# A 64-byte wider constant tile, a token scaling on VectorE and a later place for the gate projections, in a one-core hybrid encoder layer

## The chip, the cores and the metric

The kernel runs on 1 core of one Trainium2 chip. The metric is the device time of one execution in microseconds (us); 0.2% of it is about what a measurement of this kernel can tell from no change. Engines are named as in the profile: PE is TensorE (PEld its loads of the resident operand), DVE is VectorE, ACT is ScalarE, POOL is GpSimd, SP is the engine that issues the transfers (DMA).

## The reference

One layer over 1024 tokens of width 1024, in float32: a mixer of window attention and a gated delta rule (DeltaNet) on one input projection, a cross attention into 256 memory tokens, and a SwiGLU network of width 2816. Each has an RMS norm before and after it.

```python
h = _rms_norm(x, g_mix_pre[l])
proj = h @ w_in[l]
aq, ak, av, dqkv, dgate, dalpha, dbeta = jnp.split(proj, IN_SPLITS, axis=-1)
...
mix = jnp.concatenate([attn_o, dn_o], axis=-1) @ w_out[l]
x = x + _rms_norm(mix, g_mix_post[l])
c = _memory_cross_attention(_rms_norm(x, g_cross_pre[l]), _rms_norm(mem, g_mem[l]),
                            w_cq[l], w_ckv[l], w_co[l])
x = x + _rms_norm(c, g_cross_post[l])
f = _swiglu(_rms_norm(x, g_ffn_pre[l]), w_gate_up[l], w_down[l])
x = x + _rms_norm(f, g_ffn_post[l])
```

`dgate` is the gate of the DeltaNet output: `o * silu(gate)`, needed only when the delta rule has run over a token.

## The kernel before

**Number format.** Every float32 operand of a large product is split in a high and a low part (`split`: ScalarE casts the high part at L102, VectorE or GpSimd subtracts it for the low part at L103), and a product is three matmuls: high by high, high by low, low by high. Nearly all of them stream an operand of 128x512 past a resident one of 128x128. In the profile `pg<-hhi,whi` means: into the PSUM tile pg, streamed hhi, resident whi.

**Memory.** Tiles are allocated in pools, on the left side of the on-chip memory, upwards from address 0, or on the right side, downwards from the end. The pool `cst` holds constants and is the first on the left; behind it come `wp`, with the raw weights `wraw` and their parts `whi` and `wlo`, and everything that is opened later: `b0` to `b3` (tokens of the later stages and the cross attention's queries), `cph` (its probabilities), `x22` and `bhi` (the SwiGLU product), `dhl` and `t4h` (the down product). On the right lie `hhi`, `hlo` (the transposed input), `s0` (again transposed tokens) and `s0h` to `s3l` (sums of weights). `phalf` is a constant that the kernel fills and does not read.

**Stages.** (1) Norm and transposition of x. (2) Input projection (`pg`, L261), tile by tile of 128 output columns; beside it the DeltaNet preparation: `base_inverse` inverts 32x32 triangles in a chain of short VectorE operations (L534, L536, ending at L538 and L539), `levels` builds larger inverses out of them with small matmuls (L576 to L591); `attn_proj` multiplies queries and keys by cosine and sine (L729, L730, L735) and stores them; `value_proj` and `gate_proj` do the value and the gates; `window` computes window attention (`psw`, L633). (3) `scan` steps the delta rule over chunks of 128 tokens, with memory keys and values and further windows as filler. (4) `mid_gemm` (`pmg`, L1016) multiplies by `w_out`, twice for 512 tokens each, then the mid norm: residual added (L1030), sum of squares (L1033), the root on GpSimd (L162), and the token tile scaled by it (L1036). (5) Cross attention: queries `pcq` (L261), scores `pcs` (L1097), output `pco` (L1123), and `mid_gemm` by `w_co`, again twice. (6) SwiGLU: gate and up product (L1191) by a scheme with seven block products, and the down product (`block_product`, L1381, and L1474).

**What sets the order.** The work of stage (2) is issued by strings: `ORDER_1` for DeltaNet, `ORDER_2` for what follows. In them `D` is a DeltaNet projection, `P` its preparation, `B` a `base_inverse`, `L` a `levels`, `A` an `attn_proj` (A4 is the keys), `V` the `value_proj`, `G` a `gate_proj`, `W` a group of windows. The order of issue is a priority: a scheduler places each instruction on its engine's queue as early as its inputs, its tiles and the engine allow by a model of durations, so work from several stages is interleaved. The place in the queue is fixed when the program is built. All transfers are issued by the SP queue. `load_w` raises the priority of loading and splitting weights. The window pool `tw` and the levels' pool reuse memory that the second `base_inverse` holds until it ends.

The token tile is scaled before the change by

```python
nc.scalar.activation(xr, z, AF.Identity, scale=r2)
```

and the tile xr is then transposed by TensorE for the next product.

Of the kernel before, what the change touches and what calls it, by code (L numbers as in the profile page):

```python
# [10 lines left out]
F32 = mybir.dt.float32  # L11
F32R = mybir.dt.float32r
I32 = mybir.dt.int32
AF = mybir.ActivationFunctionType
ALU = mybir.AluOpType
# [4 lines left out]
P = 128  # L20
# [13 lines left out]


ORDER_1 = "D0 P0 D1 P1 D2 B0 P2 D3 P3 B1".split()
ORDER_2 = "L0 L1 G0 G1 A4 V A0 A1 L2 L3 W W W A2 A3 G2 G3 W".split()
ORDER_3 = ("M " + "s01 W K " * 5 + "s01 K " * 3 + "s01 V V").split()


# [35 lines left out]
def tile_hybrid_block(  # L76
# [6 lines left out]
    nc = tc.nc  # L83
# [4 lines left out]
    if dump is None:  # L88
        def dump(name, ap):
            pass  # L90
# [17 lines left out]
    def pool(name, bufs, **kw):  # L108
        return tc.tile_pool(name=name, bufs=bufs, reuse_waits="tile", **kw)

    cst = ctx.enter_context(pool("cst", 1))
# [6 lines left out]
    def load_w(src, k, n, eng=None, after=None):  # L118

        with tc.high_priority(AHEAD):  # L120
            raw = wp.tile([P, k, n], F32, tag="wraw", name="wraw")
            with ExitStack() as order_:
                if after:
                    order_.enter_context(tc.issue_after(after.ins))
                nc.sync.dma_start(raw, src.rearrange("(k p) n -> p k n", p=P))
            hi = wp.tile([P, k, n], F32R, tag="whi", name="whi")
            lo = wp.tile([P, k, n], F32R, tag="wlo", name="wlo")
            split(hi, lo, raw, eng=eng)
        return hi, lo
# [2 lines left out]
    ident = cst.tile([P, P], F32, name="ident")  # L132
    mhalf = cst.tile([P, 16], F32, name="mhalf")
    nc.gpsimd.memset(mhalf, -0.5)
    phalf = cst.tile([P, 16], F32, name="phalf")
    nc.gpsimd.memset(phalf, 0.5)
    cols = cst.tile([P, P], F32, name="cols")
    p12 = ExitStack()
# [19 lines left out]
    def rstd_of(rs, ss, n, eps):  # L158

        w = ss.shape[-1]  # L160
        nc.gpsimd.tensor_scalar(rs, ss, n, eps, ALU.mult, ALU.add)
        nc.gpsimd.tensor_tensor(rs, rs, mhalf[:, :w], ALU.pow)  # L162
# [540 lines left out]
    def issue(order, table):  # L703
        for o in order:
            table[o[0]](*(int(c) for c in o[1:]))
# [54 lines left out]

    issue(ORDER_2, {"A": attn_proj, "V": value_proj, "G": gate_proj, "L": levels, "W": next_windows})
    dump("d_q", d_q); dump("d_k", d_k); dump("d_gate", d_gate)
# [202 lines left out]
    L0 = ExitStack()  # L965
# [33 lines left out]
    def mid_gemm(tz, act, w, gp, res, dst, hf, between=None):  # L999


        zs = [tz.tile([P, D], F32, tag="z", name="z", bufs=4) for _ in range(4)]
        sss = [tz.tile([P, 2], F32, tag="zss", name="zss", bufs=8) for _ in range(4)]
        for ch in range(2):
            cs = slice(ch * 512, (ch + 1) * 512)
            if ch and between:
                between()
            pp = [pg.tile([P, 512], F32, tag="pg", name="pmg") for _ in range(4)]
            for kp in range(4):
                whi, wlo = load_w(w[kp * 256:(kp + 1) * 256, cs], 2, 512)  # L1010
                for t in range(4):
                    tt = slice(t * P, (t + 1) * P)
                    for kk in range(2):
                        k = 2 * kp + kk
                        for i, (w_, a) in enumerate(((whi, 0), (whi, 1), (wlo, 0))):
                            nc.tensor.matmul(pp[t], act[a][:, k, tt], w_[:, kk, :], start=(k == 0 and i == 0),  # L1016
                                             stop=(k == KT - 1 and i == 2))
            for t in range(4):
                nc.scalar.activation(zs[t][:, cs], pp[t], AF.Square, accum_out=sss[t][:, ch:ch + 1])
                nc.vector.tensor_tensor(zs[t][:, cs], pp[t], gp[:, cs], ALU.mult)  # L1020
        xn = []
        for t in range(4):
            tok = slice(hf * HALF + t * P, hf * HALF + (t + 1) * P)
            z = zs[t]
            xr = tz.tile([P, D], F32, tag="xr", name="xr", bufs=XR)
            nc.sync.dma_start(xr, res[tok, :])
            rs = tz.tile([P, 1], F32, tag="prs", name="prs", bufs=4)
            nc.gpsimd.tensor_scalar(rs, sss[t][:, 1:2], sss[t][:, 0:1], D * EPS, ALU.add, ALU.add)
            nc.gpsimd.tensor_tensor(rs, rs, mhalf[:, 0:1], ALU.pow)
            nc.vector.scalar_tensor_tensor(z, z, rs, xr, ALU.mult, ALU.add)  # L1030
            nc.sync.dma_start(dst[tok, :], z)
            s2 = tz.tile([P, 1], F32, tag="ps2", name="ps2", bufs=4)
            nc.scalar.activation(xr, z, AF.Square, accum_out=s2)  # L1033
            r2 = tz.tile([P, 1], F32, tag="pr2", name="pr2", bufs=4)
            rstd_of(r2, s2, 1.0 / D, EPS)
            nc.scalar.activation(xr, z, AF.Identity, scale=r2)  # L1036
            xn.append(xr)
        return xn

# [4 lines left out]
    L1 = ExitStack()  # L1044
# [6 lines left out]
    for hf in range(2):  # L1051
        for kp in range(4):
# [4 lines left out]
            split(mxT[hf][0][:, k2, :], mxT[hf][1][:, k2, :], raw[:, k2, :])  # L1057
    LR.close()
    xn0 = mid_gemm(tz, mxT[0], w_out, gp, x, d_x1, 0)
    h2T = [[opB.tile([P, KT, HALF], F32R, tag=b1, name=b1), opB_first[2]]]  # L1060
    xn1 = mid_gemm(tz, mxT[1], w_out, gp, x, d_x1, 1, between=lambda: turn_norm(xn0, "cross", *h2T[0], pin=True))
    h2T.append(operand(opA, "s0"))
    turn_norm(xn1, "cross", *h2T[1])
# [9 lines left out]
    L2 = ExitStack()  # L1073
# [63 lines left out]
    L3 = ExitStack()  # L1137
# [6 lines left out]
    def blocks(t):  # L1144
        return t[:, 0:HK], t[:, HK:KT]

    xn = mid_gemm(tz, q0, w_co, gp, d_x1, d_x2, 0)
    x1h, x1l = operand(opA, "s0")
    X11, X21 = (x1h[:, 0:HK], x1l[:, 0:HK]), (x1h[:, HK:KT], x1l[:, HK:KT])
# [252 lines left out]
    def residual(t, after=None):  # L1402
        xr = tp_.tile([P, D], F32, tag="xrf", name="xrf")
        with tc.issue_after((after or late).ins):
            nc.sync.dma_start(xr, d_x2[t * P:(t + 1) * P, :])
        return xr
# [57 lines left out]
    for t in range(4):  # L1464
# [14 lines left out]
        xr = residual(r)  # L1479
# [40 lines left out]
```

## Time and profile before

| | us |
|---|---|
| median of 3 runs (1558.93 to 1559.38) | 1559.16 |
| the profiled execution | 1562.86 |
| its span | 1561.1 |
| DVE busy | 1052.3 |
| ACT busy | 726.5 |

The busy times are sums over the span and say little of what limits it. The chain of waits follows the end of the program back from cause to cause; its lines by engine say which engine's time was on the path. A group of instructions by line has the count and the shortest, the middle and the longest duration; a window lists for a stretch, after its length, each engine's busy time and number of instructions, the granted clock of TensorE (1.00 is full, 0.50 half) and the share of DMA in use. In a list of durations a matmul's duration is longer than the distance to the next, since they are pipelined: 0.39 us against 0.23.

The two halves of the profile differ. The page's slices of the span have TensorE at nine tenths nearly throughout, and its clock at nine tenths or more in all of them:

```profile
PE   6999999988999999999999999999999999999998
...
PEclk9999999999999999999999999999999999999999
```

### The profile page before, as it was taken

How to read it: one execution, taken by the hardware profiler on the slowest of the kernel's cores; microseconds unless marked ns; L12 is line 12 of the kernel's file. 1: busy time of each engine (PE TensorE's matmuls, PEld its weight loads, DVE VectorE, ACT ScalarE, POOL GpSimd, SP SyncE). 2: the span in 40 equal slices, each digit the busy share in tenths (PEclk: the TensorE clock that was granted, in tenths of full speed). 3: DMA queues.
4: the chain of work that ended last, by engine and by line, in shares of the span. 5: the costliest groups of instructions: out<-in, count | busy, mean ns of one | idle time of the engine just before them, and what ended most of it. 6: DMA issues, size and time to landing. Idle time of an engine off the chain costs nothing.

```text
span 1561.1 us, 20936 instructions
## 1 busy us (share of the span) xinstructions
PE 1504.1 (96%) x7451; PEld 1252.7 (80%) x7451; DVE 1052.3 (67%) x1742; ACT 726.5 (47%) x1388; POOL 308.8 (20%) x305
## 2 busy tenths in 40 slices
PE   6999999988999999999999999999999999999998
PEld 5888787877899777888888877888888888888786
DVE  6777888767998855434346377776867554696665
ACT  6665552346557765453336574322222222454532
POOL 2000110000004102153102221443433333000021
PEclk9999999999999999999999999999999999999999
DMA  6244446868987674354213254333433334753354
GB/s 208 70 130 121 130 146 159 219 176 273 336 268 251 199 268 149 116 169 147 68 54 135 97 190 139 115 125 119 157 119 109 101 102 138 286 195 102 108 174 164
DMA packets 267367, 247.17 MB, mean 158 GB/s; under 512 B 39016, under 2 KB 204797, under 8 KB 267261
## 3 DMA queue, kind: packets, MB, share of 16 engines
q1 hardware_dynamic: 267261, 245.82, 49.6%
q8 instruction: 59, 0.97, 0.2%
q14 instruction: 47, 0.39, 0.1%
HBM read 173.65 MB, written 69.50 MB: 156 GB/s over the span
## 4 chain that ended last, share of the span: by engine, by line
PE 78%; DVE 7%; DMA 6%; ACT 3%; issue 2%; SPq 2%; POOL 1%; DVEq 0%; POOLq 0%; ACTq 0%
PE pg L261 13%; PE pmg L1016 10%; PE pD L1191 8%; PE pE L1191 8%; PE pA L1191 6%; PE pcq L261 6%; PE pdX L1381 6%; PE pdA L1381 4%; PE pB L1191 4%; PE pdD L1381 2%; PE psc L785 2%; PE pcs L1097 1%; PE pco L1123 1%; DVE wlo L103 1%; PE pdX L1474 1%
## 5 line engine op out<-in xcount | busy, mean ns | idle before, releaser
L102 ACT CAST whi<-wraw 128x1024 fp32r<-128x1024 f32 x108 | 113.1, 1048 | 170.6 <-PE pg L261 38.4
L103 DVE TENSOR_TENSOR wlo<-wraw,whi 128x1024 fp32r<-128x1024 f32 x78 | 95.5, 1225 | 87.4 <-ACT whi L102 83.3
L261 PE MATMUL pg<-hhi,whi 128*128 128x512 f32 x352 | 142.1, 405 | 1.5 <-DVE rop L730 1.5
L261 PE MATMUL pg<-hhi,wlo 128*128 128x512 f32 x352 | 141.0, 401 | 0.0
L261 PE MATMUL pg<-hlo,whi 128*128 128x512 f32 x352 | 141.0, 401 | 0.0
L1016 PE MATMUL pmg<-whi,b 128*128 128x512 f32 x384 | 120.0, 399 | 2.6 <-ACT whi L102 2.2
L1191 PE MATMUL pA<-s,whi 128*128 128x512 f32 x352 | 111.4, 397 | 1.2 <-ACT m L1208 1.2
L103 POOL TENSOR_TENSOR wlo<-wraw,whi 128x1024 fp32r<-128x1024 f32 x30 | 73.9, 2464 | 147.0 <-ACT whi L102 138.8
L1016 PEld LDWEIGHTS pmg<-whi,b 128*128 128x128 f32 x384 | 72.2, 191 | 18.2 <-ACT whi L102 2.6
L261 PEld LDWEIGHTS pg<-hhi,whi 128*128 128x128 f32 x352 | 67.0, 191 | 16.7 <-DVE rop L730 2.0
L261 PEld LDWEIGHTS pg<-hlo,whi 128*128 128x128 f32 x352 | 67.0, 190 | 14.8
L1191 PEld LDWEIGHTS pA<-s,whi 128*128 128x128 f32 x352 | 65.2, 187 | 16.8 <-ACT m L1208 1.9
L261 PEld LDWEIGHTS pg<-hhi,wlo 128*128 128x128 f32 x352 | 66.7, 190 | 14.7
L1381 PE MATMUL pdX<-dhl,whi 128*128 128x512 f32 x264 | 76.1, 390 | 1.5 <-DVE zv L1436 0.8
L1016 PE MATMUL pmg<-wlo,b 128*128 128x512 f32 x192 | 71.5, 392 | 0.0
L1191 PE MATMUL pA<-s,wlo 128*128 128x512 f32 x176 | 69.7, 397 | 1.1 <-DVE wlo L103 1.1
L102 ACT CAST whi<-araw 128x1024 fp32r<-128x1024 f32 (+1 forms) x36 | 35.3, 982 | 71.3 <-PE pdX L1381 27.6
L1268 POOL TENSOR_TENSOR act<-act,up 128x512 f32<-128x512 f32 x33 | 50.1, 1519 | 91.1 <-DVE up L1267 54.3
L103 DVE TENSOR_TENSOR wlo<-araw,whi 128x1024 fp32r<-128x1024 f32 (+1 forms) x36 | 40.8, 1133 | 40.2 <-ACT whi L102 40.2
L286 DVE SCALAR_TENSOR_TENSOR acc<-cp,cols,acc 128x1024 f32<-128x1024 f32 x48 | 61.4, 1281 | 1.5 <-ACT acc L284 0.9
L1381 PEld LDWEIGHTS pdX<-dhl,whi 128*128 128x128 f32 x264 | 49.3, 188 | 12.8 <-issue 1.1
L1241 DVE TENSOR_TENSOR sr<-sr,wraw 128x512 f32<-128x512 f32 x22 | 38.1, 1732 | 29.1 <-POOL sr L1240 29.1
(408 smaller groups left out, 3971.9 us busy)
## 6 DMA issues: line engine op xcount, KB each, us to landing
wraw<-in_w_gate_up_dram SPq DMA_DIRECT2D x52, 512.0 KB, 3.9
kv<-d_kv SPq DMA_DIRECT2D x32, 512.0 KB, 6.7
wraw<-in_w_in_dram SPq DMA_DIRECT2D x22, 512.0 KB, 4.6
b<-in_w_down_dram SPq DMA_DIRECT2D x20, 512.0 KB, 6.8
araw<-d_as SPq DMA_DIRECT2D x20, 512.0 KB, 3.6
pz<-d_pz SPq DMA_DIRECT2D x32, 256.0 KB, 6.5
wraw<-in_w_ckv_dram SPq DMA_DIRECT2D x16, 512.0 KB, 7.1
wraw<-in_w_out_dram SPq DMA_DIRECT2D x16, 512.0 KB, 4.2
```

The lines of the kernel that those rows point to most:

```text
L102: nc.scalar.copy(hi, src)
L103: (eng or nc.vector).tensor_tensor(lo, src, f32(hi), ALU.subtract)
L261: nc.tensor.matmul(p_, w[:, k, :], ah[a][:, k, :], start=(k == 0 and i == 0), stop=(k == nk - 1 and i == 2))
L286: nc.vector.scalar_tensor_tensor(acc, cp[:, t:t + S], taps[t], acc, ALU.mult, ALU.add)
L785: nc.tensor.matmul(out[:, d, h, :], lt[:, d, h, :], rt[:, d, h, :], start=True, stop=True)
L1016: nc.tensor.matmul(pp[t], act[a][:, k, tt], w_[:, kk, :], start=(k == 0 and i == 0), stop=(k == KT - 1 and i == 2))
L1097: nc.tensor.matmul(pp[:, t2_, :], q[a][:, ct, tt], kr_[b_][:, ct, :], start=(j == 0 and i == 0), stop=(j == 1 and i == 2))
L1123: nc.tensor.matmul(po, vr_[a][:, kt, cs], pts[kt][b_], start=(kt == 0 and i == 0), stop=(kt == 1 and i == 2))
L1191: nc.tensor.matmul(out_, w[a][:, k, :], xx[b_][:, k, :], start=(start and k == 0 and i == 0), stop=(k == HK - 1 and i == 2), skip_group_ch ...
L1241: nc.vector.tensor_tensor(s[1], s[0], a_[:, 0:HK], ALU.subtract)
L1268: nc.gpsimd.tensor_tensor(o_, o_, up, ALU.mult)
L1381: nc.tensor.matmul(banks[t], a[:, k - k0, tt], w, start=(first and k == 0 and i == 0), stop=(k == NB - 1 and i == 2), skip_group_check=not ...
```

## The change

Three edits. The constant tile `phalf` gets 32 floats per partition (128 bytes) and is used by its first 16. The token tiles of the mid norms are scaled by VectorE instead of ScalarE. In `ORDER_2` the gate projections stand behind all the attention projections and levels.

```diff
-ORDER_2 = "L0 L1 G0 G1 A4 V A0 A1 L2 L3 W W W A2 A3 G2 G3 W".split()
+ORDER_2 = "L0 L1 A4 A0 A1 V L2 L3 W W W A2 A3 G0 G1 G2 G3 W".split()
...
-    phalf = cst.tile([P, 16], F32, name="phalf")
+    phalf = cst.tile([P, 32], F32, name="phalf")[:, 0:16]
     nc.gpsimd.memset(phalf, 0.5)
...
             rstd_of(r2, s2, 1.0 / D, EPS)
-            nc.scalar.activation(xr, z, AF.Identity, scale=r2)
+            nc.vector.tensor_scalar(xr, z, r2, None, ALU.mult)
```

The first edit alone leaves each engine's queue as it was. The other two move instructions. Three places follow; a row is an instruction with its line, and a sign says whether it stands only in the queue before (-) or only in the changed one (+).

VectorE at the first mid norm (z is the sum with the residual, xr the scaled tile, wlo the low part of the next weights):

```order
 L103 TENSOR_TENSOR wlo<-wraw,whi 128x1024
 L1020 TENSOR_TENSOR z<-pmg,gpost 128x512
-L1030 SCALAR_TENSOR_TENSOR z<-z,prs,xr 128x1024 x2
+L1030 SCALAR_TENSOR_TENSOR z<-z,prs,xr 128x1024
+L1036 TENSOR_SCALAR xr<-z,pr_6330 128x1024
+L1030 SCALAR_TENSOR_TENSOR z<-z,prs,xr 128x1024
+L1036 TENSOR_SCALAR xr<-z,pr_6343 128x1024
+L1036 TENSOR_SCALAR xr<-z,pr_6356 128x1024
+L1036 TENSOR_SCALAR xr<-z,pr_6369 128x1024
 L103 TENSOR_TENSOR wlo<-wraw,whi 128x1024 x3
```

The four scalings stand between the residual sums and three low parts of weights. ScalarE at the same place:

```order
 L1033 ACTIVATE xr,ps_6328<-z 128x1024
 L1033 ACTIVATE xr,ps_6341<-z 128x1024
-L1036 ACTIVATE xr<-z,pr_6330 128x1024
-L1036 ACTIVATE xr<-z,pr_6343 128x1024
 L1033 ACTIVATE xr,ps_6354<-z 128x1024
 L1033 ACTIVATE xr,ps_6367<-z 128x1024
-L1036 ACTIVATE xr<-z,pr_6356 128x1024
-L1036 ACTIVATE xr<-z,pr_6369 128x1024
 L102 CAST whi<-wraw 128x1024 x3
```

The casts of the next weights follow the sums of squares directly. VectorE inside the first `base_inverse` (L534 and L536 are its chain; sn, rop and rot are tiles of the rotation of queries and keys):

```order
 L286 SCALAR_TENSOR_TENSOR acc<-cp,cols,acc 128x1024
 L534 TENSOR_TENSOR tmpb<-A 128x240
-L457 TENSOR_TENSOR gm<-glo,C 128x512
+L735 TENSOR_TENSOR rop<-rop,rot_2428 128x512
+L729 TENSOR_TENSOR sn<-pg,sinT 128x512
+L730 TENSOR_TENSOR rop<-pg,cosT 128x512
 L536 TENSOR_TENSOR A<-A,tmpb 128x16x15
+L103 TENSOR_TENSOR wlo<-wraw,whi 128x1024
+L103 TENSOR_TENSOR qlo<-rop,qhi 128x512
 L534 TENSOR_TENSOR tmpb<-A 128x240
```

The rotation, which stood behind this chain, now stands between its steps. In TensorE's queue the first window matmul (L633) has 116 projection matmuls of stage (2) behind it before the change and 51 with it.

## The prediction

> **What bounds the kernel now.** I read the page's busy times first, then the chain of waits (the run of work that ended last, followed backwards).
>
> ```profile
> span 1561.1 us, 20936 instructions
> PE 1504.1 (96%) x7451; PEld 1252.7 (80%) x7451; DVE 1052.3 (67%) x1742; ACT 726.5 (47%) x1388; POOL 308.8 (20%) x305
> ...
> PE 78%; DVE 7%; DMA 6%; ACT 3%; issue 2%; SPq 2%; POOL 1%; DVEq 0%; POOLq 0%; ACTq 0%
> ```
>
> TensorE works 1504 of 1561 us, and 78% of the chain is its own. So two things can move the time: TensorE's waits, some 57 us in all, and the time of one matmul, of which there are thousands. For the second I read the chain in order of time. Each row gives start, duration, line and count of an unbroken run of matmuls, all of them 128x512; duration over count is the spacing.
>
> ```profile
> 48.40 7.45 PE pg L315 x32
> ...
> 232.22 21.94 PE pg L261 x94
> ...
> 695.16 5.46 PE pcq L261 x24
> ...
> 761.43 6.30 PE pcq L261 x27
> ...
> 888.84 14.33 PE pmg L1016 x63
> ...
> 1341.17 59.84 PE pdA L1381 x264
> ```
>
> The same view cut to two shorter stretches:
>
> ```profile
> 727.79 2.32 PE pco L1123 x10
> ...
> 1047.28 2.75 PE pD L1191 x12
> 1050.03 2.72 PE pE L1191 x12
> 1052.74 2.80 PE pA L1191 x12
> 1055.55 2.80 PE pB L1191 x12
> ```
>
> Equal instructions run at two rates. pdA has 59.84/264 = 226.7 ns each, pmg 227.5, the first pcq run 227.5, pE 226.7; the projections pg have 233.4, the second pcq run 233.3, pA 233.3. Laid beside the built program's table of addresses, they sort themselves. Where both operands start at a multiple of 256 bytes (whi, wlo, b0 to b3, dhl: all on the left side of the memory), it is 226.7 to 227.5. Where the streamed operand lies on the right side (hhi, hlo and the pair s0, all 448 bytes past a multiple of 512), it is 233.4. pco streams cph, on the left but 128 past a multiple of 256: 232.0. L315 has neither operand on a multiple: 232.8. With only the resident operand off a multiple (the weight sums of pD and pB) the rate is 229.2 or 233.3. So I read the start address of the streamed operand as the cause, the memory's side as accidental.
>
> **The tile.** phalf is 64 bytes wider, and every left-side tile allocated after it stands 64 bytes higher (whi 25856 to 25920, b0 42240 to 42304, dhl 64768 to 64832): from multiples of 256 to 64 past one. The right side stays. With this edit alone no instruction changes its place, so its cost is spacing only. How many matmuls stream a left tile: L1381, L1474, L1016 between 612 and 905 us (the three calls of mid_gemm with a resident operand in b0 to b3), the first cross_q at L261, and the gate-up products, in this order; last, from the page's costliest groups, one of the three equal groups of projections:
>
> ```profile
> 0.00:1561.00 1561.00, 180.45 (x792) 148.42 (x792) 0.99 0.50 158
> 0.00:1561.00 1561.00, 30.55 (x132) 24.62 (x132) 0.99 0.50 158
> 612.00:905.00 293.00, 140.46 (x577) 107.26 (x575) 0.99 0.35 118
> 663.00:713.00 50.00, 45.72 (x192) 35.40 (x192) 1.00 0.62 206
> 970.00:1340.00 370.00, 370.00 (x1604) 301.22 (x1603) 249.82 (x307) 111.14 (x178) 139.25 (x86) 1.00 0.39 125
> ...
> L261 PE MATMUL pg<-hhi,whi 128*128 128x512 f32 x352 | 142.1, 405 | 1.5 <-DVE rop L730 1.5
> ```
>
> If 64 past 256 costs what 448 past 512 does: the down products 792 + 132 = 924 x (233.4 - 226.7) = 6.2 us; L1016 577 x (233.4 - 227.5) = 3.4; cross_q 192 x 5.9 = 1.1; the gate-up stretch, a mixture at 370/1604 = 230.7 now, 1604 x 2.7 = 4.3. I add 1.5 for what has no row here (L1016 before 612, where the resident operand is already off, the scores, the memory keys, the short stretch of gate-up before 970): an estimate, a tenth of the rest. Sum +16.5. Bounds: 0, if the address isn't the cause, and +27.5, if a misplaced resident operand adds its 2.75/12 - 2.72/12 = 2.5 ns on top for the 3,297 matmuls counted above and the 3 x 352 projections, whose resident operand moves off its multiple too; L315, with both off at 232.8, speaks against that. I take +16.5. VectorE's and ScalarE's times show no dependence on the address that I could find.
>
> **The token tiles.** L1036 scales four 128x1024 tiles in each of four norms, on ScalarE now. Views: timeline of ScalarE and of TensorE, a window of that stretch, and the groups of L1036 and of L894, which is the same operation on VectorE.
>
> ```profile
> 622.05 2.18 ACT L1036 ACTIVATE xr<-z,pr 128x1024 f32<-128x1024 f32 x2
> 624.14 1.98 ACT L102 CAST whi<-wraw 128x1024 fp32r<-128x1024 f32 x2
> ...
> 625.22 3.66 PE L1016 MATMUL pmg<-whi,b 128*128 128x512 f32 x8 [2.18 <-ACT whi L102]
> ...
> 625.20:628.60 3.40, 3.38 (x8) 2.70 (x9) 2.36 (x2) 0.92 (x1) 0.00 (x0) 0.50 0.21 63
> ...
> L1036 ACT ACTIVATE xr<-z,pr x16: 1132/1152/1158, 617.4 to 917.7; 128x1024 f32<-128x1024 f32 x16
> ...
> L894 DVE TENSOR_SCALAR mt<-mt,mrs x2: 746/750/753, 379.9 to 381.3; 128x1024 f32<-128x1024 f32 x2
> ```
>
> So 16 x 1.15 = 18.4 us leave ScalarE and 16 x 0.75 = 12 us come to VectorE, nearly all beside matmuls. On the path lies one place: two scalings stand before the cast of the next weights, TensorE waits 2.18 us for it and then runs 3.40 us at half the clock, which loses 3.4 x 0.5 = 1.7. Up to 3.9 us can go. Near 913 to 921 us three smaller waits of 0.5 us on the same engines could go as well: at best -5.5. Against it: VectorE now runs four scalings (3.0 us), the last of which waits for GpSimd's root, and behind them stand three low parts wlo, which TensorE needs; a new wait of up to 2 us would outweigh part of it. I take -3.5, near the wait that is measured; bounds -5.5 and +2.
>
> The Trainium skill (TensorE: Matmul & The Clock Gate, "What's actually happening") has the clock drop after an idle window of about 3.4 us. By that a wait of 2.18 us should not halve the clock, and only about -1.8 would be left here; the trace shows 0.50 right behind the wait, so I keep to the trace.
>
> **The order.** Now the projections A0 to A4 and V stand before the gates. Rows: VectorE's rotary operations (L729; L730 and L735 are like it), the last step of the triangular inverse (L539), the levels behind it (L591), the first window matmul (L633), TensorE's waits in the stage, and two windows at half clock.
>
> ```profile
> L729 DVE TENSOR_TENSOR sn<-pg,sinT x10: 681/684/692, 235.8 to 335.7; 128x512 f32<-128x512 f32 x10
> ...
> L539 DVE TENSOR_TENSOR A<-A,bB x2: 1225/1226/1226, 232.3 to 297.5; 128x1024 f32<-128x1024 f32 x2
> ...
> L591 PE MATMUL ps<-bs,D x128: 191/275/403, 257.2 to 371.2; 128*128 128x32 f32 x64, 128*128 128x64 f32 x64
> ...
> L633 PEld LDWEIGHTS psw<-khi,qs x64: 186/192/336, 315.2 to 545.8; 128*128 128x128 f32 x64
> ...
> PE psw L633 <- DMA qs<-d_q: 3.7, 1, 3.7
> ...
> PE ptv L749 <- ACT vT L746: 1.8, 1, 1.8
> PE pg L261 <- DVE rop L730: 1.5, 1, 1.5
> ...
> 260.00:266.80 6.80, 6.80 (x22) 5.89 (x23) 6.39 (x20) 3.72 (x11) 0.00 (x0) 0.50 0.52 135
> 314.60:318.00 3.40, 2.82 (x9) 2.36 (x10) 0.92 (x4) 0.00 (x0) 0.00 (x0) 0.50 1.16 321
> ```
>
> No work is added; it is moved. The attention tiles are done early, so the first windows no longer wait for their queries on the DMA, and 3.7 + 1.8 + 1.5 of waits and 6.8 x 0.5 + 3.4 x 0.5 = 5.1 of half clock may vanish: -12.1 at best. Given back: some 25 rotary operations of 0.69 us (17 us of VectorE) now stand inside the chain of the first inverse, which ended with L539 at 232.3, and 76 more projection matmuls (17.7 us) run before the levels begin. Behind them, the levels of the second head pair, which ran beside 112 projection matmuls from 318 to 371, have only 25 left: 87 x 0.2334 = 20 us of cover are gone. Window matmuls fill about half, so up to +10 of idle. Between -12 and +10 neither end is nearer to a row; I take +1.
>
> **Sum.** +16.5 - 3.5 + 1 = +14 on the profiled execution's 1562.86 us (its span 1561.1 and 1.8 around it), 3.7 above the median of the runs. On the median 1559.2 that is **1573 us**.
>
> **Rivals.** Stationary penalties add (+27.5 in place of +16.5): 1584; L315 speaks against it. The windows come late: levels and windows idle TensorE for the full +10, so 1559.2 + 16.5 - 3.5 + 10 = 1582; for it the lost cover, against it that the scan stage behind takes up window work that is late.
>
> On the other side: **the tile costs nothing.** Where the matmuls stream left tiles, the cause of 233.4 may be the offset between the two operands, and tiles that move together keep it; all rows above but L315 would fit, since fast pairs share one side. Then the other edits alone decide: 1559.2 - 3.5 + 1 = 1556.7, and with the order's waits all closed 1559.2 - 3.5 - 12.1 = 1543.6. The kernel becomes faster from the point at which the tile costs under 2.5 us. The Trainium skill leads here too: a matmul's gap there is its columns plus a fixed cost, 215.7 ns at 512 columns whatever the address (TensorE: Matmul & The Clock Gate, "Wait — 56ns, not 53.3ns?"), and SBUF has lines of 16 bytes, of which 64 is a multiple (SBUF — State Buffer, "Specifications (TRN2)"). The trace with its 226.7 and 233.4 agrees with neither page so far.
>
> **Numbers.** The forecast 64%, added penalties 8%, late windows 8%, a tile that costs nothing 20% (13 of them near 1556.7, 7 near 1543.6). A change of 0.2%, 3.1 us, is about what can be told from none. Faster: the 7, half of the 13 and 1 of the forecast's lower tail, 14%; the same: 6% from around 1557; slower: 80%. The forecast's own range is 1565 to 1582 (tile +9 to +20, the other two -3 to +3); the range for 8 in 10 reaches from 1556, which takes in the upper half of the costless tile, to 1586.
>
> **What would show it.** Right: pdA's run in the chain near 233 ns a matmul instead of 226.7, the first cross_q and L1016 like it, the gate-up stretch over 233, and projections as now at 233.4; ScalarE's scaling gone from before the cast near 622 and no 2.18 us wait there; in the stage of the attention a first L633 earlier than 315. Wrong: pdA still at 226.7 (then the offset or the side decides, and the time falls to about 1557), or the down products over 235 (penalties add); a wait of TensorE for wlo behind VectorE's four scalings; long waits of TensorE at L591 between 320 and 380.

## The result and the profile after

The changed kernel takes 1577.22 us (median of 4 runs, 1573.73 to 1578.96) against 1559.27: a ratio of 1.0102 (95% interval 1.0081 to 1.0123), slower. The time is 4 us from the forecast of 1573, inside its range, and the sign is right. The trace shows at once that the terms behind it are not. The page's busy times of the changed kernel:

```profile
span 1575.6 us, 20942 instructions
...
PE 1511.7 (96%) x7451; PEld 1255.2 (80%) x7451; DVE 1068.3 (68%) x1758; ACT 706.1 (45%) x1370; POOL 311.2 (20%) x305
```

TensorE is busy 7.6 us longer and the span of the profiled execution is 14.5 us longer, so about half of that is new idle time. The chain of waits in order of time, for the matmuls on which the largest term rested:

```profile
1018.09 2.80 PE pE L1191 x12
...
1355.44 59.84 PE pdA L1381 x264
```

This run of the gate-up product pE, with weight sums as the resident operand, has 2.80/12 = 233.3 ns; over 1000 to 1300 us a gate-up product takes 300/1293 = 232.0 ns (300/1301 = 230.6 before), where over 233 was forecast. But pdA, whose two operands both moved by 64 bytes, has 59.84/264 = 226.7 ns, the figure of before to the digit. The start address of the streamed operand does not set the rate.

Where the time went can be read from when stages begin. First the last step of each inverse (L539), the levels (L591), the first windows (L633) and one group of the scan's matmuls (L785), in the changed kernel; the row's two times behind the durations are the first and the last start:

```profile
L539 DVE TENSOR_TENSOR A<-A,bB x2: 1225/1225/1225, 253.0 to 311.5; 128x1024 f32<-128x1024 f32 x2
...
L591 PE MATMUL ps<-bs,D x128: 190/276/421, 280.6 to 388.2; 128*128 128x32 f32 x64, 128*128 128x64 f32 x64
...
L633 PE MATMUL psw<-khi,qs x64: 277/340/670, 330.5 to 560.2; 128*128 128x384 f32 x48, 128*128 128x256 f32 x16
...
L785 PE MATMUL psc<-kv,pz x128: 272/275/377, 397.5 to 525.8; 128*128 128x128 f32 x128
```

The same group of the scan before:

```profile
L785 PE MATMUL psc<-kv,pz x128: 270/275/377, 382.9 to 510.8; 128*128 128x128 f32 x128
```

The last step of the first inverse starts 20.7 us later than before (253.0 against 232.3), the levels begin 23.4 us later (257.2 before), the first windows 15.3 us later, the scan 14.6. So the loss of the profiled execution is there when the scan begins. VectorE from the first to the last step of that inverse, before and changed:

```profile
168.40:233.60 65.20, 60.37 (x127) 1.00 0.49 147
```

```profile
167.80:254.30 86.50, 78.31 (x156) 1.00 0.57 165
```

The inverse takes 21.3 us longer, and 29 more instructions stand in it, 17.9 us of VectorE's time; 18 of them, 12.4 us, are the rotation (six each of L729, L730 and L735). A window of TensorE over the stage, before and changed:

```profile
200.00:440.00 240.00, 225.19 (x1334) 0.97 0.77 227
```

```profile
200.00:440.00 240.00, 217.85 (x1212) 0.94 0.72 203
```

TensorE is busy 7.3 us less in the same 240 us, and its granted clock is lower. The stretches at half clock in the changed kernel, each with busy time and matmuls:

```profile
276.60:280.00 3.40, 3.40 (x10) 0.50 1.15 302
327.80:334.60 6.80, 4.11 (x12) 0.50 1.03 227
355.10:361.90 6.80, 4.58 (x14) 0.50 0.17 51
379.00:389.20 10.20, 10.06 (x42) 0.50 0.31 90
409.70:413.10 3.40, 3.40 (x19) 0.50 1.05 405
```

They are 30.6 us against 13.6 before (the two that the prediction shows and one of 3.4 at 379.5), and TensorE is busy in 25.55 us of them against 13.02. So 12.5 us more of its work ran at half clock, which loses half of that, 6.3 us. With the 7.3 us of idle that is 13.6, about the 14.6 by which the scan is late.

### The profile page after: what moved, and what is told of

It reads as the page before. It is cut to its first block, busy times and chain, and to the rows that moved or that the text cites. A ratio compares the mean times of both kernels' runs of the same rounds, so it can differ in the third digit from the quotient of the medians.

```text
span 1575.6 us, 20942 instructions
## 1 busy us (share of the span) xinstructions
PE 1511.7 (96%) x7451; PEld 1255.2 (80%) x7451; DVE 1068.3 (68%) x1758; ACT 706.1 (45%) x1370; POOL 311.2 (20%) x305
```

## The experiments

In all of them, times are compared with runs of the kernel before on the same chip.

**Each edit alone, and the other side of the memory.** The first three kernels have one of the three edits each. The wider tile moves addresses alone: the kernel does read `phalf`, as an exponent in the DeltaNet preparation (L470), but the four columns that it reads keep their values. The fourth kernel has none of the edits and moves the right side instead:

```diff
-    nc.gpsimd.memset(off.tile([P, 8], F32, name="off"), 0.0)
+    nc.gpsimd.memset(off.tile([P, 56], F32, name="off"), 0.0)
```

> Only the wider constant tile. Theory 1 (the offset between the streamed and the resident operand, taken modulo 256 bytes, sets the matmul's spacing: equal offsets 227 ns, unequal 232 to 233): down products stay at 226.8 ns, projections go from 233.3 to about 232.5, the gate-up products with weight sums resident rise from 229-231 to about 232.8; the time rises by 2 to 4 us. Theory 2 (the streamed operand's own start address, as forecast): down products go to 233 ns and the time rises by 16 us.

> Only the token tiles of the mid norms on VectorE. Theory 1 (the wait of the first mid norm goes and little comes back): 3 to 5 us faster than before. Theory 2 (four scalings on VectorE delay low parts of weights and transpositions as much as ScalarE is relieved): within 1 us of before.

> Only the gate projections behind the attention projections. Theory 1 (the inverse is delayed by rotary work on VectorE, levels and windows run without cover): 13 to 17 us slower than before, the first L591 near 280 us instead of 257, the first scan matmul L785 near 397 instead of 383. Theory 2 (the order alone is worth little, +1, and the loss needs the wider tile's slower matmuls): within 4 us of before.

> Before, with the first tile on the right side widened from 32 to 224 bytes, so that the right side too starts at multiples of 256 bytes; no instruction moves. Both address theories: projections from 233.3 to 227 ns (1056 matmuls, -6.5 us), half of cross_q -1.2 us, gate-up from 230.7 to 227 ns (1604 matmuls, -6 us); in all 12 to 15 us faster. If the memory's side and not the offset decides: no change.

| kernel | ratio to before | 95% interval | us, of 1559.3 |
|---|---|---|---|
| only_tile | 1.0051 | 1.0038 to 1.0064 | +8 |
| only_scaling | 0.9985 | 0.9975 to 0.9996 | -2.3 |
| only_order | 1.0078 | 1.0065 to 1.0090 | +12.2 |
| right_side_256 | 0.9944 | 0.9929 to 0.9960 | -8.7 |

The three add up to +17.9, the change's own +18. Of the forecasts, only_order came out a little under its 13 to 17 us, with the levels at 284.4 us and the scan at 398.1 as its first theory had them. only_scaling lies between its two theories; only_tile met neither time (2 to 4 us, or 16), and right_side_256 gained less than the 12 to 15 us that it was to gain. What each does is in the traces.

*The tile.* The chain of only_tile, a long run of projections and the down product, and a window of 300 us in the gate-up products:

```profile
233.00 21.92 PE pg L261 x94
...
1344.52 59.84 PE pdA L1381 x264
...
1000.00:1300.00 300.00, 300.00 (x1293) 1.00 0.37 119
```

Projections stay slow (233.2 ns), the down products fast, and the gate-up products go from 230.6 to 300/1293 = 232.0 ns. Of right_side_256 the same two views:

```profile
228.76 21.37 PE pg L261 x94
...
1000.00:1300.00 300.00, 300.00 (x1325) 1.00 0.37 118
```

Here projections take 227.3 ns and gate-up products 226.4. The right side was 448 bytes past a multiple of 512, the left 256 past one; with the right side at 256 as well, the slow rate is gone nearly everywhere. pco stays slow (2.33 us for 10); its two operands, both on the left, still differ by 128. In only_tile both operands of the down products moved and they stayed fast; with one operand left behind, 64 against 192, the gate-up products became slower. So the difference of the two start addresses decides, not an address. How much it costs varies: pD, with only the weight sums off, had 229.2 ns before, and in only_tile a run of pE with both operands 64 past a multiple, between runs of unequal pairs, has 2.76/12 = 230.0. In right_side_256 all four kinds of gate-up product have 226.7. The 3.6 us by which the span of only_tile's profiled execution is longer (1564.7 against 1561.1) nearly fit these rates: 1848 gate-up matmuls x 1.4 ns = 2.6 us, and 0.3 us in the first product of w_out (119 matmuls in 27.93 us instead of 27.68). The timed runs say 6 to 10 us. Part of the rest is which executions were profiled: that of before took 1562.86, 1.5 above the median of the runs beside only_tile (1561.4), that of only_tile 1566.46, 1.2 below its own (1567.7). What a longer execution loses, and so the rest of the +8, no trace shows.

right_side_256 falls short of its forecast where projections are: its pmg run of 63 begins 5.8 us earlier than before (883.09 against 888.84), where 7.7 were forecast for projections and cross_q, and pdA 11.1 us earlier (1330.09 against 1341.17).

*The scaling.* In the first norm the wait of 2.18 us and its half clock are gone, and TensorE's instructions run 3.9 us earlier behind it, against those ahead of it. The second norm shows a new price: between 664 and 700 us they lose 3.3 us again. VectorE's and GpSimd's timelines of only_scaling, and TensorE's beside them:

```profile
671.51 2.87 DVE L1036 TENSOR_SCALAR xr<-z,pr 128x1024 f32<-128x1024 f32 x1 [0.44 <-POOL pr L162]
...
675.10 2.88 DVE L1036 TENSOR_SCALAR xr<-z,pr 128x1024 f32<-128x1024 f32 x1
```

```profile
671.45 2.38 POOL L103 TENSOR_TENSOR wlo<-wraw,whi 128x1024 fp32r<-128x1024 f32 x1
...
675.03 2.40 POOL L103 TENSOR_TENSOR wlo<-wraw,whi 128x1024 fp32r<-128x1024 f32 x1
```

```profile
674.43 0.44 PE L985 MATMUL ptn<-ident,xr 128*128 128x128 f32 x2 [1.08 <-DVE xr L1036]
```

An operation of 0.75 us takes 2.87 us when a low part of weights on GpSimd began 0.06 us before it: that is 2.12 us more, nearly what was left of the 2.38, as if it had waited for the other's end. The transpositions behind it wait 1.08 and 0.96 us. The Trainium skill (SBUF — State Buffer, "Who interferes with whom") says that VectorE and GpSimd share a pair of ports as an exclusive lock which `tensor_scalar` can need, and that the later one is blocked for the whole instruction; these rows agree with it.

**Is it the offset, and is it the rotation?** The fifth kernel has the wider constant tile and the right side moved by 128 bytes, so that both sides are 64 past a multiple of 256. The next two leave out the rotation of queries and keys, without and with the late gates:

```diff
-            nc.vector.tensor_tensor(sn, pp[hf], sinT[:, sl], ALU.mult)
-            nc.vector.tensor_tensor(rop, pp[hf], cosT[:, sl], ALU.mult)
...
-                nc.sync.dma_start(rot[32 * q:32 * q + 32], sn[o:o + 32])
-            nc.vector.tensor_tensor(rop, rop, rot, ALU.add)
+            nc.scalar.copy(rop, pp[hf])
```

The eighth joins what had helped, with ScalarE kept for the norm that stands beside GpSimd's work (the second call for w_out):

```diff
-            nc.scalar.activation(xr, z, AF.Identity, scale=r2)
+            nc.scalar.activation(xr, z, AF.Identity, scale=r2) if dst is d_x1 and hf else nc.vector.tensor_scalar(xr, z, r2, None, ALU.mult)
```

> The wider constant tile of the change, and the first tile on the right side widened from 32 to 160 bytes, so that both sides start 64 past a multiple of 256; no instruction moves. Theory 1 (equal offsets modulo 256 make a matmul fast, wherever they are): projections and gate-up products at 227 ns, as with the right side at 256, and 8 to 12 us faster than before. Theory 2 (only multiples of 256 are fast): everything at 232 to 233 ns, 15 us or more slower than before.

> Before, with the rotary multiplication left out: queries and keys are copied by ScalarE, so 30 operations of 0.69 us leave VectorE and their small transfers the queue. The partner of late_gates_no_rotation. Expected 0 to 6 us faster than before, since the rotation stood behind the first inverse.

> The gates behind the attention projections, and the rotary multiplication left out in the same way. Theory 1 (the order costs because rotary work on VectorE delays the first inverse): at most 4 us slower than no_rotation, first L591 within 6 us of its. Theory 2 (the order costs by itself, since gates are late or projections are used up before the levels): 10 us or more slower than no_rotation.

> The right side at multiples of 256 with the constant tile and the order of before, and the token tiles scaled by VectorE in three of the four mid norms (ScalarE where the next transpositions stand between the first query products, 673 to 677 us). Theory 1 (2.2 us of wait and 1.7 of half clock go in the first norm, the two waits of 1 us at L985 do not come): right_side_256 less 3 to 5 us, so 12 to 15 us faster than before. Theory 2 (the scaling on VectorE is worth nothing): as right_side_256, 9 to 11 us.

| kernel | ratio to before | 95% interval |
|---|---|---|
| tile_and_right_64 | 0.9950 | 0.9933 to 0.9967 |
| no_rotation | 0.9985 | 0.9972 to 0.9998 |
| late_gates_no_rotation | 0.9960 | 0.9949 to 0.9972 |
| best | 0.9876 | 0.9857 to 0.9896 |

With the changed constant tile and neither side at a multiple of 256, tile_and_right_64 is as fast as right_side_256. Its chain has

```profile
228.72 21.34 PE pg L261 x94
```

227.0 ns a projection. So equal offsets are what counts, and multiples of 256 are not.

Without the rotation the late gates cost nothing; they gain some 4 us (0.9960 against 0.9985, the intervals just meet). The end of the inverse and the begin of the levels, without and with the late gates:

```profile
L539 DVE TENSOR_TENSOR A<-A,bB x2: 1226/1226/1226, 231.8 to 279.2; 128x1024 f32<-128x1024 f32 x2
...
L591 PE MATMUL ps<-bs,D x128: 190/275/276, 258.9 to 365.9; 128*128 128x32 f32 x64, 128*128 128x64 f32 x64
```

```profile
L539 DVE TENSOR_TENSOR A<-A,bB x2: 1200/1218/1235, 236.4 to 284.5; 128x1024 f32<-128x1024 f32 x2
...
L591 PE MATMUL ps<-bs,D x128: 191/275/323, 262.3 to 364.7; 128*128 128x32 f32 x64, 128*128 128x64 f32 x64
```

The levels begin 3.4 us later instead of 27.2 (284.4 in only_order, 257.2 before). The rotation leaves the DMA queue too, and the queries are plain copies, so this pair removes some 20 us of VectorE's work and the waits for these transfers at the same time; which of the two counts most it doesn't tell apart.

The kernel best is 1.24% faster than before, 19.3 us where 12 to 15 were forecast, and faster than right_side_256 and only_scaling, whose gains it joins: its profiled span is 1542.2 against 1549.6 of right_side_256. Against right_side_256, TensorE's instructions run 2.4 us earlier behind the first norm, and another 5.3 us earlier by 1000 us, where three waits of 0.5 to 0.6 us and one of 2.0 with a period of half clock are gone. Its scalings, on VectorE none over 0.76 us:

```profile
L1036 DVE TENSOR_SCALAR xr<-z,pr x12: 745/754/756, 614.1 to 906.0; 128x1024 f32<-128x1024 f32 x12
...
L1036 ACT ACTIVATE xr<-z,pr x4: 1137/1152/1157, 663.2 to 670.2; 128x1024 f32<-128x1024 f32 x4
```

**The rotation elsewhere, and how wide equal is.** Three of the last four kernels take the rotation off VectorE with nothing left out (ScalarE copies the product, GpSimd multiplies and adds): with the late gates, in best, and in best with the late gates. The fourth shifts the right side once more, its first tile now 480 bytes wide. The edit of the rotation:

```diff
-            nc.vector.tensor_tensor(sn, pp[hf], sinT[:, sl], ALU.mult)
-            nc.vector.tensor_tensor(rop, pp[hf], cosT[:, sl], ALU.mult)
+            nc.scalar.copy(rop, pp[hf])
+            nc.gpsimd.tensor_tensor(sn, rop, sinT[:, sl], ALU.mult)
+            nc.gpsimd.tensor_tensor(rop, rop, cosT[:, sl], ALU.mult)
...
-            nc.vector.tensor_tensor(rop, rop, rot, ALU.add)
+            nc.gpsimd.tensor_tensor(rop, rop, rot, ALU.add)
```

> The late gates of the change, with the rotation of queries and keys taken off VectorE and nothing left out: ScalarE copies the product from PSUM, GpSimd does the two multiplications and the sum. Theory 1 (the late gates cost because the rotation on VectorE delays the first inverse): first L591 within 6 us of before's 257 and the time at most 4 us over before, below only_order by 8 us or more. Theory 2 (the order costs by itself): as only_order, 10 us or more over before.

> The kernel of the run best, with the rotation on GpSimd in the same way and the order of before. Theory 1: within 3 us of best, since the rotation stood behind the first inverse there and GpSimd is slower with it. Partner of best_late_gates.

> best_gpsimd with the late gates. Theory 1 (late gates leave more projections as cover once the inverse is not delayed): 0 to 6 us faster than best_gpsimd. Theory 2: 10 us or more slower.

> As right_side_256, with the right side's first tile at 480 bytes: the right side starts at multiples of 512 and the left 256 past one. Theory 1a (the offset counts modulo 256): projections at 228 ns and the time as right_side_256, 8 to 12 us faster than before. Theory 1b (it counts modulo 512): projections at 232 to 233 ns, and about the time of before.

| kernel | ratio to before | 95% interval |
|---|---|---|
| late_gates_gpsimd | 1.0121 | 1.0100 to 1.0143 |
| best_gpsimd | 0.9982 | 0.9970 to 0.9993 |
| best_late_gates | 1.0015 | 1.0005 to 1.0025 |
| right_side_0 | 0.9932 | 0.9911 to 0.9953 |

The first three missed their forecasts. GpSimd costs best 1.06% by itself, and the late gates 0.33% on top, where a gain was expected. The first inverse of late_gates_gpsimd shows one reason. The rows are VectorE's windows over it for L534 alone and for L536 alone, its last step, TensorE's wait for the first levels, and TensorE's window behind that wait:

```profile
169.90:247.40 77.50, 13.39 (x30) 0.98 0.50 151
169.90:247.40 77.50, 13.42 (x30) 0.98 0.50 151
...
L539 DVE TENSOR_TENSOR A<-A,bB x2: 1224/1651/2078, 246.1 to 302.5; 128x1024 f32<-128x1024 f32 x2
...
PE ps L585 <- DMA m<-d_inv: 5.4, 1, 5.4
...
266.00:283.10 17.10, 15.34 (x66) 0.50 0.44 102
```

The inverse is still 13.8 us late (246.1 against 232.3). With GpSimd's multiplications beside it the 60 short steps of its chain take 26.8 us instead of 19.7 before. TensorE waits 5.4 us for the first levels and then has half clock for 17.1 us. best_late_gates has the same two, a wait of 8.0 us and 20.5 us of half clock from 259.5. In best_gpsimd, with the order of before, TensorE's longest wait of the stage is a new one of 6.3 us, for VectorE (`m`, L635) ahead of a window; the rest of its 1.06% was not followed. So this set neither supports nor refutes that the rotation on VectorE alone is the cause; it moved the work onto an engine that gets in VectorE's way. The pair without rotation stands as the evidence.

right_side_0 is as fast as right_side_256 within the intervals; its chain has

```profile
229.08 21.37 PE pg L261 x94
```

227.3 ns a projection with the two operands 256 bytes apart modulo 512. Here offsets count modulo 256.

## Why the prediction came out right

The number and the sign were right; two of three terms were mis-sized in opposite directions, so the sum fits by chance.

**What bounds the kernel** held: the two rates of equal matmuls, and TensorE's waits with the half clock beside them, are where the differences were found. The reading of the cause failed. The sentence "I read the start address of the streamed operand as the cause" is wrong; the difference of the two start addresses modulo 256 is the cause. The rival "the tile costs nothing" had this cause, with 20%, and its sign, pdA still at 226.7, came; the time did not fall to that rival's 1557, since the order cost 12 us and not 1. The rows of before allowed both readings. I let L315 speak against the offset, since both its operands lie on the right side; but they start at 448 and at 320 past a multiple of 512, which differ by 128. With that, the rows that the prediction shows at 226.7 to 227.5 have equal offsets and those at 232 and over unequal ones; pD at 229.2, with unequal ones, lies between.

**The tile**, +16.5: measured +8 (6 to 10). The step that failed is "If 64 past 256 costs what 448 past 512 does": the down products' 6.2, the 3.4 of mid_gemm from 612 us on and cross_q's 1.1 did not come (in only_tile pmg has 14.35/63 = 227.8 ns and the first pcq 5.47/24 = 227.9), and of the gate-up products' 4.3 only 2.6. It was mainly products with one operand on each side that became slower, and part of the measured size has no row.

**The token tiles**, -3.5: measured -2.3 (-3.9 to -0.6). The mechanism at 622 us was right to the wait and to its half clock, 3.9 us. That the half clock goes with the wait is not certain, though: right_side_256 has the same wait, 2.24 us, and a granted clock of 1.00 behind it, so there the edit had less to gain (2.4 us in best). The price was put in the wrong place: not a wait for wlo behind four scalings in the first norm, but scalings held up beside GpSimd in the second, 2.0 us of waits and 3.3 us in all.

**The order**, +1: measured +12.2 (10.1 to 14.0), just past the +10 that the rival of late windows had. The steps were named (rotation inside the inverse's chain, levels late, cover gone), though the first window matmul came at 330.5 us and not ahead of 315. The failing step is "Between -12 and +10 neither end is nearer to a row; I take +1". The cover lost was read from rows; that the waits of before would close had no row, and the one for the queries on the DMA became 6.4 us instead of 3.7, as TensorE's waits in the changed kernel show:

```profile
PE pow L664 <- ACT ph L102: 6.5, 3, 2.8
PE psw L633 <- DMA qs<-d_q: 6.4, 1, 6.4
...
PE ps L585 <- DVE mov L603: 2.1, 2, 1.9
PE ps L585 <- DMA m<-d_inv: 1.9, 1, 1.9
```

The idle time grew by 7.3 us, within the +10. What the bound did not hold is the half clock that came with five of the gaps, 6.3 us more than before.

## What to carry to other kernels

Equal matmuls that follow one another at 227 and at 233 ns pointed to the start addresses here: compare streamed and resident operand modulo 256, and shift a whole side of the memory by a dummy tile; that was worth 0.6% here and moves no instruction. Work that is moved earlier is paid on the engine where a chain of short dependent operations runs: count the instructions that come to stand between its steps. Before VectorE takes over an operation, look at what GpSimd does at that time.

## What the runs showed of the hardware that was not expected

A matmul whose two operands start at different offsets modulo 256 took 232 to 233 ns instead of 226.7 in most of these streams, whichever side they lie on; with only the resident operand off a multiple of 256 it was 229.2 in some. A `tensor_scalar` on VectorE took 2.87 us instead of 0.75 beside a 2.38 us operation of GpSimd. In the changed kernel's attention stage five waits of TensorE of 1.9 to 6.4 us came with half clock for one to three periods of 3.4 us, and waits of 0.9 and 1.2 us did not; the added half clock cost 6.3 us, nearly as much as the added idle time (7.3 us). Whether a wait of 2.2 us brings it varied: at the first mid norm the clock behind it was 0.50 before and in tile_and_right_64, 1.00 in only_tile and right_side_256.
